# The forget sum of an attention's logits, moved from four-row matmuls into a zero row of the keys

## The chip, the cores and the metric

The program runs on one core of a Trainium2 chip: TensorE (PE; its weight loads are listed as PEld), VectorE (DVE), ScalarE (ACT), GpSimd (POOL) and SyncE (SP), which here only issues DMAs. The metric is the device time of one execution in microseconds (us).

## The reference

A sequence of 256 tokens with 1024 features passes two layers of a first block and two layers of a second one (gated linear recurrence and windowed attention). A layer of the first block is a SwiGLU, a mixer, and a SwiGLU. The mixer has four groups of 256 features each: differential attention, a convolution of 31 taps, a chunked spatial gate, and the forgetting attention, which is the one that is changed:

```python
def _forgetting_attention(q, k, v, log_f):      # four heads of 64
    cum = jnp.cumsum(log_f.astype(jnp.float32), axis=1)
    ...
        s = jnp.einsum('bqhd,bkhd->bhqk', qi, k).astype(jnp.float32) * scale
        s = s + jnp.transpose(ci, (0, 2, 1))[..., None] - cum_k[:, :, None, :]
        ...
        p = jax.nn.softmax(jnp.where(causal, s, NEG_INF), axis=-1)
        return jnp.einsum('bhqk,bkhd->bqhd', p.astype(v.dtype), v)
```

The term of the query's own position (`ci`) is the same for all keys, so the softmax drops it, and only the key's running sum is needed: one number for each head and key.

## The kernel before, in words

**Tiling.** Every large product is fp32 split into a high and a low part: three matmuls (L368 high by high, L369 activations' high by weights' low, L370 low by high) for each 128x512 product, summed in one PSUM bank. Weights stream from HBM in pieces of 512 KB (`wr`, issued on SP, three buffers). ScalarE casts each piece to its high part (`wh`, L336) and VectorE subtracts to get the low part (`wl`, L339), both into nine buffers.

**A mixer layer.** The input product yields column groups in the order conv, dqk, fqk, vv, gmlp. Each of the four mixer groups is a Python generator that is advanced between pieces of the large product, so that its small work stands among the weight matmuls. A scheduler with priorities then fixes the order on each engine, and an engine runs its list strictly in order. The output product takes the groups in the order differential attention, forgetting attention, spatial gate, convolution (`OUT1 = [0, 3, 2, 1]`), so it can't end before the convolution's features are there. The convolution's 62 taps (L875) run on VectorE wherever the order puts them. Behind them come transposes (L884), a layer norm (L845, L846, then L444 and small instructions), ScalarE's `L852`, transposes (L626), and a split into high and low (L336 on ScalarE, L339 on VectorE) for the output product. The weights of the spatial gate and its products (L917 to L920) come before that.

**The forgetting attention (`fox`).** q and k of a token half are normalised, transposed on PE (L489) and copied from PSUM by ScalarE: k to `kT` (L1033, two heads above one another in 128 partitions), q to `qm` (L1036) twice, each time multiplied by a column `mg` that is the gain in one head's 64 rows and zero in the other's. So the product of `qm` and `kT` over 128 rows holds one head alone. For each head PE adds into one PSUM bank the causal mask (L1046), the running sum `cum` (4 rows by 256, made by `decay`) by a matmul over four rows in which a broadcast column of the identity picks the head (L1049), and the product of q and k (L1051). `exp_rows` takes the row maximum on VectorE (L647) and the exponentials on ScalarE (L651). Small constants of all groups lie in one tile, `col_sb`, of 880 columns, loaded by one DMA at the start.

Of the kernel before, what the change touches and what calls it, by code (L numbers as in the profile page):

```python
# [9 lines left out]
F32 = mybir.dt.float32  # L10
# [3 lines left out]
AF = mybir.ActivationFunctionType  # L14
# [4 lines left out]
S, D, DEPTH, DFF = 256, 1024, 2, 2816  # L19
# [21 lines left out]
Z1 = [(n, Z1_COLS[n]) for n in ("conv", "dqk", "fqk", "vv", "gmlp")]  # L41
OUT1 = [0, 3, 2, 1]
MIX1 = ("diff", "conv", "gmlp", "fox")

_PERM = [(2048 + 64 * h, 2112 + 64 * h) for i in range(4) for h in (i, i + 4)]
Z2 = [
# [90 lines left out]
_F1 = {}  # L137
for _name, _n in [("ada_b", 144), ("norm_g", 48), ("conv_w", 124), ("conv_b", 4), ("conv_g", 4), ("conv_nb", 4),
                  ("dgq", 2), ("dgk", 2), ("dog", 2), ("fgq", 2), ("fgk", 2), ("bs", 8), ("fb", 2),
                  ("lam", 256), ("maskf", 2), ("ident", 128), ("tri", 128), ("hgain", 2), ("sink", 16)]:  # L140
    _off = sum(n for _, n in _F1.values())
    _F1[_name] = (_off, _n)
NCOL = sum(n for _, n in _F1.values())
# [2 lines left out]
def pack_cols(inp):  # L146
    out = np.zeros((128, NCOL), np.float32)

    def put(name, a):
        o, n = _F1[name]  # L150
        out[:a.shape[0], o:o + n] = a.reshape(a.shape[0], n)

    def fm(a):
        return a.reshape(-1, 128).T

    def rep(a, k):
        return np.concatenate([a] * k, axis=-1)

    put("ada_b", fm(inp["ada_b"]))
    put("norm_g", fm(inp["norm_g"]))  # L160
    put("conv_w", inp["conv_w"].reshape(2, TAPS, 2, 128).transpose(3, 0, 2, 1))
    put("conv_b", fm(inp["conv_b"]))
    put("conv_g", fm(inp["conv_norm_g"]))
    put("conv_nb", fm(inp["conv_norm_b"]))
    put("dgq", rep(inp["diff_qk_g"][:, 0], 4).T)
    put("dgk", rep(inp["diff_qk_g"][:, 1], 4).T)
    put("dog", rep(inp["diff_out_g"], 2).T)
    put("fgq", rep(inp["fox_qk_g"][:, 0], 2).T)
    put("fgk", rep(inp["fox_qk_g"][:, 1], 2).T)
    put("bs", inp["gmlp_bs"].transpose(2, 0, 1))  # L170
    put("fb", inp["fox_fb"].T)
    put("lam", np.broadcast_to(inp["diff_lambda"].reshape(1, 256), (128, 256)))
    p = np.arange(128)
    put("maskf", (p[:, None] // 64 == np.arange(2)[None]).astype(np.float32))
    put("ident", np.eye(128, dtype=np.float32))
    put("tri", (p[:, None] <= p[None, :]).astype(np.float32))
    put("hgain", inp["hgrn_head_gain_2"].T)
    sk = inp["attn_sinks_2"].reshape(1, 2, 2, 4).transpose(0, 1, 3, 2)
    put("sink", np.broadcast_to(sk.reshape(1, 16), (128, 16)))
    return out  # L180
# [43 lines left out]
def body(ctx, tc, ws, cols, x, c, adaw, wf, gmn, wst, bmask, lev, pred, sbias, gains, lbs, out, phases=range(12)):  # L224
    nc = tc.nc
    V, A, T = nc.vector, nc.scalar, nc.tensor
# [5 lines left out]
    def nm(p):  # L232
        uid[0] += 1
        return f"{p}{uid[0]}"

    def pool(name, bufs=1, stack=ctx, **kw):
        return stack.enter_context(tc.tile_pool(name=name, bufs=bufs, **kw))

    const = pool("const")
# [9 lines left out]
    def s2(shape=(128, 512), dt=F32):  # L249
        return s2_p.tile(list(shape), dt, tag="s2", name=nm("s"))  # L250

    def s1(shape=(128, 256), dt=F32):
        return s1_p.tile(list(shape), dt, tag="s1", name=nm("h"))

    def sm(n):
        return sm_p.tile([128, 32], F32, tag="sm", name=nm("m"))[:, 0:n]

    def tp(shape, dt=F32):
        return ps_p.tile(list(shape), dt, tag="ps", name=nm("t"))
# [13 lines left out]
    def C(name, i=0, n=None):  # L273
        o, w = _F1[name]
        return col_sb[:, o + i:o + (w if n is None else i + n)]

    ident = C("ident")
# [208 lines left out]
    def transposed(src):  # L486
        ps = tp([128, 4, 128])
        for j in range(4):
            T.transpose(ps[:, j], src[:, 128 * j:128 * j + 128], ident)  # L489
        return ps  # L490
# [138 lines left out]
    def bc(ap, n):  # L629
        return ap.unsqueeze(2).to_broadcast([ap.shape[0], ap.shape[1], n])  # L630

    def heads(ap, e):
        return ap.rearrange("p (g e) -> p g e", e=e)
# [21 lines left out]
    def keys_first(p):  # L655

        ps = tp([128, 4, 128])
        for i in range(4):
            T.transpose(ps[:, i], p[i], ident)
        pt = s2([128, 4, 128])  # L660
        A.copy(pt, ps)
        return pt
# [2 lines left out]
    first_block = ctx.enter_context(ExitStack())  # L665
    mod = [const.tile([128, 72], F32, name=f"mod{l}") for l in range(2)]
    an = [const.tile([128, 24], F32, name=f"an{l}") for l in range(2)]
    const.tile([128, 8], F32, name="trail")
    c1 = pool("c1", 1, first_block)
    ada_p = pool("ada", NA, first_block)  # L670
    cond = c1.tile([128, D], F32, name="cond")
# [154 lines left out]
    def mix1(ph):  # L826
        l = ph // 3
        got = {}
        mg, cvh, ypad = G1["mg"], G1["cvh"], G1["ypad"]
# [95 lines left out]
        def qk_norms(acc, group):  # L925

            n = 512 // group
            r = sm(2 * n)
            res = [s2(), s2()]
            for t in range(2):  # L930
                A.activation(res[t], acc[t], AF.Square)
                V.tensor_reduce(out=r[:, n * t:n * t + n], in_=heads(res[t], group), axis=AX.X, op=ALU.add)
            rsqrt(r, r, 1.0 / group)
            for t in range(2):
                V.tensor_tensor(out=heads(res[t], group), in0=heads(acc[t], group),
                                in1=bc(r[:, n * t:n * t + n], group), op=ALU.mult)
            return res
# [70 lines left out]
        def decay():  # L1008

            ps = tp([4, S])  # L1010
            wfh, wfl = G1["wf"]
            for k in range(8):
                mm3(ps, wfh[:, l, k], wfl[:, l, k], xh[:, k], xl[:, k], k == 0, k == 7)
            y, e, cum = s1()[0:4], s1()[0:4], s1()[0:4]
            fb = C("fb", l, 1)[0:4]
            V.tensor_scalar(out=y, in0=ps, scalar1=fb, scalar2=0.0, op0=ALU.add, op1=ALU.min)
            A.activation(e, ps, AF.Abs, bias=fb)
            A.activation(e, e, AF.Exp, scale=-1.0)
            A.activation(e, e, AF.Ln, bias=1.0)
            V.tensor_tensor(out=e, in0=e, in1=y, op=ALU.subtract)  # L1020
            V.tensor_tensor_scan(out=cum, data0=G1["ones"], data1=e, initial=0.0, op0=ALU.mult, op1=ALU.add)
            return cum

        def fox(acc):
            zs = qk_norms(acc, 64)
            cum = decay()
            yield
            yield
            kT = s2([128, 2, S])
            qm = []  # L1030
            for t in range(2):
                ps = transposed(zs[t])
                A.copy(kT[:, :, 128 * t:128 * t + 128], ps[:, 2:4])  # L1033
                q = s2([128, 2, 2, 128])
                for i in range(2):
                    A.activation(q[:, :, i], ps[:, 0:2], AF.Copy, scale=mg[:, l, 1 + i:2 + i])  # L1036
                qm.append(q)
            yield
            p, r = [[], []], []
            for t in range(2):  # L1040
                keys = 128 * (t + 1)
                per = 512 // keys
                sums = sm(4)
                for b in range(4 // per):
                    ps = tp([128, per, keys])
                    T.matmul(ps.rearrange("p a b -> p (a b)"), identb, G1["mask"][t], start=True, stop=False)  # L1046
                    for i in range(per):
                        g = b * per + i
                        T.matmul(ps[:, i], ident[0:4, g:g + 1].to_broadcast([4, 128]), cum[:, 0:keys], start=False,  # L1049
                                 stop=False)  # L1050
                        T.matmul(ps[:, i], qm[t][:, g // 2, g % 2], kT[:, g // 2, 0:keys], start=False,  # L1051
                                 stop=i == per - 1)
                    p[t] += exp_rows(ps, per, sm(per), sums, range(b * per, b * per + per))
                    yield
                r.append(sm(4))
                V.reciprocal(out=r[t], in_=sums)
            yield
            pts = [[keys_first([p[t][i][:, 128 * kt:128 * kt + 128] for i in range(4)]) for kt in range(t + 1)]
                   for t in range(2)]
            yield  # L1060
            while ("v", 0) not in got:
                yield
            o = [s1(), s1()]
            for t in range(2):
                ps = weighted(pts[t], [got["v", n][:, 256:512] for n in range(2)])
                V.tensor_tensor(out=heads(o[t], 64), in0=ps, in1=bc(r[t], 64), op=ALU.mult)
            yield
            got["fox"] = mixed_slot(to_features(o))
# [15 lines left out]
        def src(i):  # L1084
            name = MIX1[OUT1[i]]
            until(lambda: name in got)
# [413 lines left out]
```

## Time and profile before

| what | value |
|---|---|
| time, median of three runs | 2214.31 us (2215.36, 2205.01, 2214.31) |
| the profiled execution's time | 2208.89 us |
| its span in the trace | 2207.1 us |
| PE busy | 2149.9 us, 97% of the span |
| VectorE busy | 1486.1 us, 67% |
| ScalarE busy | 1191.5 us, 54% |
| mean granted TensorE clock | 0.991 |

The profiled execution's time is 1.8 us over its span, which begins with the first instruction on the engines. A matmul's listed length runs past the start of the next one, since they are pipelined. What a matmul costs PE is the distance from one start to the next. A granted clock of 1.00 is the full 2.4 GHz, 0.50 the lower level of 1.2 GHz.

### The profile page before, as it was taken

How to read it: one execution, taken by the hardware profiler on the slowest of the kernel's cores; microseconds unless marked ns; L12 is line 12 of the kernel's file. 1: busy time of each engine (PE TensorE's matmuls, PEld its weight loads, DVE VectorE, ACT ScalarE, POOL GpSimd, SP SyncE). 2: the span in 40 equal slices, each digit the busy share in tenths (PEclk: the TensorE clock that was granted, in tenths of full speed). 3: DMA queues.
4: the chain of work that ended last, by engine and by line, in shares of the span. 5: the costliest groups of instructions: out<-in, count | busy, mean ns of one | idle time of the engine just before them, and what ended most of it. 6: DMA issues, size and time to landing. Idle time of an engine off the chain costs nothing.

```text
span 2207.1 us, 27771 instructions
## 1 busy us (share of the span) xinstructions
PE 2149.9 (97%) x10148; PEld 1765.8 (80%) x10150; DVE 1486.1 (67%) x2224; ACT 1191.5 (54%) x1933; POOL 0.2 (0%) x4
## 2 busy tenths in 40 slices
PE   6999998999999999999999999999999999999998
PEld 5787776888888777888888888888888887887887
DVE  6788986765888786655754665675566557657653
ACT  6544656544544756553644565464465447556552
POOL 0000000000000000000000000000000000000000
PEclk9999998999999999999999999999999999999999
DMA  8889734885889533755755543475555555245652
GB/s 321 294 318 337 259 118 152 293 265 174 314 336 342 209 113 126 247 181 183 246 187 188 179 143 115 135 234 184 191 181 202 189 171 183 96 143 177 205 182 95
DMA packets 125416, 452.90 MB, mean 205 GB/s; under 512 B 14176, under 2 KB 14432, under 8 KB 125280
## 3 DMA queue, kind: packets, MB, share of 16 engines
q1 hardware_dynamic: 125280, 451.13, 59.2%
q8 instruction: 80, 1.31, 0.2%
q14 instruction: 56, 0.46, 0.1%
HBM read 450.03 MB, written 1.05 MB: 204 GB/s over the span
## 4 chain that ended last, share of the span: by engine, by line
PE 77%; DMA 8%; ACT 7%; DVE 6%; issue 2%; SPq 0%; DVEq 0%; ACTq 0%
PE a L368 23%; PE a L369 22%; PE a L370 22%; DMA wr<-in_ws 8%; ACT wh L336 3%; DVE wl L339 3%; PE t L626 2%; PE t L489 1%; PE t L1234 1%; ACT h L476 1%; DVE spill L683 1%; ACT s L533 1%; PE t L1188 1%; PE t L970 1%; PE t L1346 0%
## 5 line engine op out<-in xcount | busy, mean ns | idle before, releaser
L339 DVE TENSOR_TENSOR wl<-wr,wh 128x1024 fp32r<-128x1024 f32 x692 | 843.2, 1223 | 468.0 <-ACT wh L336 463.0
L336 ACT CAST wh<-wr 128x1024 fp32r<-128x1024 f32 x692 | 726.8, 1052 | 718.5 <-PE a L370 388.1
L368 PE MATMUL a<-wh,xh 128*128 128x512 f32 x1888 | 750.7, 398 | 7.9 <-ACT xh L534 6.0
L369 PE MATMUL a<-wl,xh 128*128 128x512 f32 x1888 | 736.4, 390 | 1.9 <-DVE wl L339 1.9
L370 PE MATMUL a<-wh,xl 128*128 128x512 f32 x1888 | 736.0, 391 | 0.0
L368 PEld LDWEIGHTS a<-wh,xh 128*128 128x128 f32 x1888 | 357.6, 189 | 81.6 <-ACT xh L534 6.7
L370 PEld LDWEIGHTS a<-wh,xl 128*128 128x128 f32 x1888 | 356.9, 189 | 75.5 <-DVE xl L339 1.4
L369 PEld LDWEIGHTS a<-wl,xh 128*128 128x128 f32 x1888 | 357.6, 189 | 73.0 <-DVE wl L339 3.7
L368 PE MATMUL a<-wh,s 128*128 128x512 f32 x896 | 352.2, 393 | 3.9 <-ACT s L336 2.8
L369 PE MATMUL a<-wl,s 128*128 128x512 f32 x896 | 350.8, 392 | 0.8 <-DVE wl L339 0.8
L370 PE MATMUL a<-wh,s 128*128 128x512 f32 x896 | 349.3, 391 | 0.0
L368 PEld LDWEIGHTS a<-wh,s 128*128 128x128 f32 x896 | 168.9, 188 | 39.8 <-ACT s L336 3.4
L369 PEld LDWEIGHTS a<-wl,s 128*128 128x128 f32 x896 | 168.9, 188 | 35.6 <-DVE wl L339 1.6
L370 PEld LDWEIGHTS a<-wh,s 128*128 128x128 f32 x896 | 168.7, 188 | 35.3 <-DVE s L339 0.6
L683 DVE CUSTOM_DVE_ANT_0 spill<-ada,cond 128x1024 bf16<-128x1024 f32 x144 | 175.5, 1219 | 5.9 <-DMA ada<-in_adaw 5.3
L489 PE MATMUL t<-col_sb,s 128*128 128x128 f32 x304 | 45.9, 285 | 27.3 <-ACT s L740 18.3
L489 PEld LDWEIGHTS t<-col_sb,s 128*128 128x128 f32 x304 | 35.1, 144 | 41.7 <-ACT s L740 19.1
L339 DVE TENSOR_TENSOR s<-t,s 128x512 fp32r<-128x512 f32 x96 | 64.9, 684 | 3.4 <-ACT s L336 3.4
L626 PE MATMUL t<-col_sb,h 128*128 128x128 f32 x392 | 58.9, 274 | 6.2 <-DVE h L594 3.2
L626 PEld LDWEIGHTS t<-col_sb,h 128*128 128x128 f32 x392 | 48.0, 141 | 19.6 <-DVE h L594 4.3
L590 ACT ACTIVATE h<-a,m 128x256 f32<-128x256 f32 x88 | 40.7, 473 | 36.4 <-PE a L370 36.3
L336 ACT CAST s<-t 128x512 fp32r<-128x512 f32 x96 | 54.9, 582 | 5.6 <-PE t L626 5.6
(241 smaller groups left out, 1251.5 us busy)
## 6 DMA issues: line engine op xcount, KB each, us to landing
wr<-in_ws SPq DMA_DIRECT2D x692, 512.0 KB, 4.0
ada<-in_adaw SPq DMA_DIRECT2D x144, 512.0 KB, 5.7
row<-in_gains SPq DMA_DIRECT2D x12, 512.0 KB, 4.9
h<-in_x SPq DMA_DIRECT2D x2, 512.0 KB, 7.3
out<-h SPq DMA_DIRECT2D x4, 256.0 KB, 2.0
cond<-in_c SPq DMA_DIRECT2D x1, 512.0 KB, 4.3
gmn<-in_gmn SPq DMA_DIRECT2D x2, 256.0 KB, 5.1
wst<-in_wst SPq DMA_DIRECT2D x2, 256.0 KB, 6.2
```

The costliest lines, as they stand in the source:

```text
L336: ins = A.copy(dst_h, src)
L339: return V.tensor_tensor(out=dst_l, in0=src, in1=dst_h.bitcast(F32), op=ALU.subtract)
L368: T.matmul(acc, a, wh, start=start, stop=False)
L369: T.matmul(acc, a, wl, start=False, stop=False)
L370: T.matmul(acc, b, wh, start=False, stop=stop)
L476: A.activation(junk, src, AF.Square, accum_out=ss[:, i:i + 1])
L489: T.transpose(ps[:, j], src[:, 128 * j:128 * j + 128], ident)
L533: A.activation(xt[:, j], ps[:, j], AF.Identity, scale=a, bias=b)
L590: A.activation(g, acc[t][:, 0:256], AF.Silu, scale=r)
L626: T.transpose(ps[:, i, 128 * t:128 * t + 128], src[t][:, 128 * i:128 * i + 128], ident)
L683: ins = V.tensor_tensor_reduce(out=spill, in0=raw, in1=cond, scale=1.0, scalar=0.0, op0=ALU.mult, op1=ALU.add, accum_out=mod[l][:, n:n + 1])
L970: T.matmul(ps[:, i], qT[rs, i, ts], kT[rs, i, 0:keys], start=False, stop=i == 1)
```

## The change

The running sum no longer has matmuls of its own. `qm` has rows that are zero for each head, and the product over 128 rows adds nothing there. In the changed kernel one of these rows holds a 1 in the queries and the running sum in the keys.

- There are two key tiles, one for even heads and one for odd ones, so `kT` is copied twice (four copies a layer, for two).
- `qm` is written by eight instructions of 128x128 a layer (scale and a bias column `frow`), for four of 128x256.
- One matmul over four rows (`frep`, 128 columns, 256 keys) writes the running sum of each head into 32 rows of a PSUM tile, and four ScalarE copies of 32x256 put them over zero rows of the keys (head 1 in rows 0 to 31, head 3 in 32 to 63, head 0 in 64 to 95, head 2 in 96 to 127).
- The eight matmuls of L1049 in a layer are gone. Every other product is as it was.
- `col_sb` has 1012 columns, for 880. A pad of 8 columns beside other constants is one of 4.

```diff
--- before
+++ after
+FOX_AT = (1, 3, 0, 2)
...
-                  ("lam", 256), ("maskf", 2), ("ident", 128), ("tri", 128), ("hgain", 2), ("sink", 16)]:
+                  ("lam", 256), ("maskf", 2), ("ident", 128), ("tri", 128), ("hgain", 2), ("sink", 16),
+                  ("frow", 4), ("frep", 128)]:
...
+    put("frep", (np.repeat(FOX_AT, 32)[None] == np.arange(4)[:, None]).astype(np.float32))
+    put("frow", (np.arange(128)[:, None] == 32 * np.argsort(FOX_AT)[None]).astype(np.float32))
...
-    const.tile([128, 8], F32, name="trail")
+    const.tile([128, 4], F32, name="trail")
...
-            kT = s2([128, 2, S])
+            kT = [s2([128, 2, S]) for _ in range(2)]
             qm = []
             for t in range(2):
                 ps = transposed(zs[t])
-                A.copy(kT[:, :, 128 * t:128 * t + 128], ps[:, 2:4])
                 q = s2([128, 2, 2, 128])
                 for i in range(2):
-                    A.activation(q[:, :, i], ps[:, 0:2], AF.Copy, scale=mg[:, l, 1 + i:2 + i])
+                    A.copy(kT[i][:, :, 128 * t:128 * t + 128], ps[:, 2:4])
+                    for n in range(2):
+                        A.activation(q[:, n, i], ps[:, n], AF.Identity, scale=mg[:, l, 1 + i:2 + i],
+                                     bias=C("frow", 2 * n + i, 1))
                 qm.append(q)
+            ps = tp([128, S])
+            T.matmul(ps, C("frep")[0:4], cum, start=True, stop=True)
+            for at, g in enumerate(FOX_AT):
+                rs = slice(32 * at, 32 * at + 32)
+                A.copy(kT[g % 2][rs, g // 2], ps[rs])
             yield
...
                         g = b * per + i
-                        T.matmul(ps[:, i], ident[0:4, g:g + 1].to_broadcast([4, 128]), cum[:, 0:keys], start=False,
-                                 stop=False)
-                        T.matmul(ps[:, i], qm[t][:, g // 2, g % 2], kT[:, g // 2, 0:keys], start=False,
+                        T.matmul(ps[:, i], qm[t][:, g // 2, g % 2], kT[g % 2][:, g // 2, 0:keys], start=False,
                                  stop=i == per - 1)
```

Line numbers behind the new lines move: L368 to L370 are L374 to L376 in the changed kernel, L336 and L339 are L342 and L345, L651 is L657, L1046 is L1060 and L1051 is L1063.

The scheduler moves other instructions with it. On PE in layer 0, where the logits of the first token half stand, before (`t_2485` is the PSUM tile of its four heads, `h_2348` the running sum, `a_...` the sums of the large product):

```order
L1046 MATMUL t_2485<-bm,identb 128x512
L1049 MATMUL t_2485<-h_2348,col_sb 128x128
L368 MATMUL a_2355<-wh_2231,xh 128x512
L369 MATMUL a_2355<-wl_2232,xh 128x512
L370 MATMUL a_2355<-wh_2231,xl 128x512
L368 MATMUL a_2356<-wh_2231,xh 128x512
L1051 MATMUL t_2485<-s_2428,s_2435 128x128
L1049 MATMUL t_2485<-h_2348,col_sb 128x128
L1051 MATMUL t_2485<-s_2428,s_2435 128x128
L1049 MATMUL t_2485<-h_2348,col_sb 128x128
L1051 MATMUL t_2485<-s_2428,s_2435 128x128
L1049 MATMUL t_2485<-h_2348,col_sb 128x128
```

and in the changed kernel (the first token half is now `t_2498`, the second half's first two heads `t_2539`):

```order
L973 LDWEIGHTS identb
L973 MATMUL t_2527<-bm,identb 128x512
L976 MATMUL t_2527<-s_2207,s_2208 128x256 x2
L1060 LDWEIGHTS identb
L1060 MATMUL t_2539<-bm,identb 128x512
L374 MATMUL a_2552<-wh_2359,xh 128x512
L375 MATMUL a_2552<-wl_2360,xh 128x512
L376 MATMUL a_2552<-wh_2359,xl 128x512
L1063 MATMUL t_2498<-s_2428,s_2435 128x128
L1063 MATMUL t_2498<-s_2429,s_2435 128x128
L1063 MATMUL t_2498<-s_2428,s_2435 128x128
L1063 MATMUL t_2498<-s_2429,s_2435 128x128
```

The four products of q and k stand close together now. The mask of their own tile (`t_2498`) is 12 weight matmuls, a differential block (L973, L976), the next tile's mask (L1060, here) and three weight matmuls ahead of the first of them. The new `frep` matmul stands further ahead, right behind the transposes of q and k.

On ScalarE at the same place of layer 0, before (`t_2429` and `t_2438` are the transposed q and k of the two token halves):

```order
L1033 COPY s_2428<-t_2429 128x2x128
L1036 ACTIVATE s_2435<-t_2429,mg 128x2x128 x2
L1033 COPY s_2428<-t_2438 128x2x128
L1036 ACTIVATE s_2444<-t_2438,mg 128x2x128 x2
L336 CAST wh_2555<-wr_2553 128x1024
L651 ACTIVATE s_2480,m_2393<-t_2475,m_2479 128x256 x2
```

and in the changed kernel (`t_2454` is the running sum spread over 32-row groups):

```order
L1042 COPY s_2428<-t_2430 128x2x128
L1044 ACTIVATE s_2435<-t_2430,col_sb,mg 128x128 x2
L1042 COPY s_2429<-t_2430 128x2x128
L1044 ACTIVATE s_2435<-t_2430,col_sb,mg 128x128 x2
L1042 COPY s_2428<-t_2442 128x2x128
L1044 ACTIVATE s_2447<-t_2442,col_sb,mg 128x128 x2
L1042 COPY s_2429<-t_2442 128x2x128
L1044 ACTIVATE s_2447<-t_2442,col_sb,mg 128x128 x2
L1051 COPY s_2429<-t_2454 32x256 x2
L1051 COPY s_2428<-t_2454 32x256 x2
L657 ACTIVATE s_2493,m_2393<-t_2488,m_2492 128x256 x2
L342 CAST wh_2562<-wr_2560 128x1024
```

Six instructions have become sixteen, and the weight cast that stood right behind them now stands behind two exponentials of the differential attention.

On VectorE at the convolution's layer norm in layer 1, before (`t_7302` is its transposed output, `s_7251` the low part of a group for the output product):

```order
L339 TENSOR_TENSOR wl_7339<-wr_7336,wh_7338 128x1024
L845 BN_STATS m_7310<-t_7302 128x6
L339 TENSOR_TENSOR s_7251<-t_7245,s_7250 128x512
L846 BN_AGGR m_7307<-m_7310 128x2
L845 BN_STATS m_7313<-t_7302 128x6
L846 BN_AGGR m_7307<-m_7313 128x2
L444 TENSOR_SCALAR m_7316<-m_7307 128x2
```

and in the changed kernel (there `t_7312`):

```order
L345 TENSOR_TENSOR wl_7303<-wr_7300,wh_7302 128x1024
L851 BN_STATS m_7320<-t_7312 128x6
L345 TENSOR_TENSOR s_7261<-t_7255,s_7260 128x512
L852 BN_AGGR m_7317<-m_7320 128x2
L851 BN_STATS m_7323<-t_7312 128x6
L345 TENSOR_TENSOR wl_7349<-wr_7346,wh_7348 128x1024
L852 BN_AGGR m_7317<-m_7323 128x2
L345 TENSOR_TENSOR wl_7355<-wr_7352,wh_7354 128x1024
L450 TENSOR_SCALAR m_7326<-m_7317 128x2
```

Two weight subtractions have moved in between the second statistics and the small instructions of the norm. Further ahead in layer 1, one more weight subtraction and one more tap stand ahead of the spatial gate's products than before. In layer 0, VectorE's four taps and a weight subtraction stand ahead of the first maximum of the forgetting attention, where the taps stood behind it. SP issues the same DMAs in nearly the same order.

## Rows read from the trace of the kernel before

**Rows 1.** The page's first line, busy times (part 1), GB/s of 40 slices (part 2).

```profile
span 2207.1 us, 27771 instructions
...
PE 2149.9 (97%) x10148; PEld 1765.8 (80%) x10150; DVE 1486.1 (67%) x2224; ACT 1191.5 (54%) x1933; POOL 0.2 (0%) x4
...
GB/s 321 294 318 337 259 118 152 293 265 174 314 336 342 209 113 126 247 181 183 246 187 188 179 143 115 135 234 184 191 181 202 189 171 183 96 143 177 205 182 95
```

**Rows 2.** Source view of L1049: durations in ns (min/median/max), first and last start.

```profile
L1049 PE MATMUL t<-h,col_sb x32: 270/374/577, 279.3 to 808.3; 4*128 4x128 f32 x16, 4*128 4x256 f32 x16
```

**Rows 3.** PE timeline, layer 0: start, length, engine, line, operation; two records a matmul.

```profile
279.31 0.48 PE L1049 MATMUL t<-h,col_sb 4*128 4x128 f32 x2
...
281.09 0.48 PE L1049 MATMUL t<-h,col_sb 4*128 4x128 f32 x2
281.50 0.49 PE L1051 MATMUL t<-s,s 128*128 128x128 f32 x2
...
285.34 0.39 PE L967 MATMUL t<-bm,identb 128*128 128x512 bf16 x1
...
287.03 0.69 PE L1049 MATMUL t<-h,col_sb 4*128 4x256 f32 x2
287.66 0.70 PE L1051 MATMUL t<-s,s 128*128 128x256 f32 x2
```

**Rows 4.** ScalarE timeline, layer 0; in brackets the idle time and what ended it.

```profile
229.71 1.85 ACT L533 ACTIVATE s<-t,mod,an 128x128 f32<-128x128 f32 x5 [2.02 <-PE t L489]
...
278.69 0.37 ACT L1033 COPY s<-t 128x256 f32<-128x256 f32 x1
...
282.21 1.04 ACT L336 CAST wh<-wr 128x1024 fp32r<-128x1024 f32 x1 [1.41 <-DMA wr<-in_ws]
```

**Rows 5.** VectorE timeline, layer 0.

```profile
283.69 0.69 DVE L647 TENSOR_REDUCE m<-t 128x4 f32<-128x512 f32 x1 [1.50 <-PE t L1051]
...
287.43 1.22 DVE L339 TENSOR_TENSOR wl<-wr,wh 128x1024 fp32r<-128x1024 f32 x1
...
322.95 2.06 DVE L875 SCALAR_TENSOR_TENSOR s<-ypad,col_sb,s 128x256 f32<-128x256 f32 x5
...
330.05 0.17 DVE L846 BATCH_NORM_AGGREGATE m<-m 128x2 f32<-128x6 f32 x1
```

**Rows 6.** PE timeline, end of layer 0's mixer.

```profile
334.56 0.44 PE L626 MATMUL t<-col_sb,h 128*128 128x128 f32 x2 [2.36 <-ACT h L852]
...
339.87 0.79 PE L368 MATMUL a<-wh,s 128*128 128x512 f32 x1 [2.77 <-ACT s L336]
...
345.15 0.39 PE L368 MATMUL a<-wh,s 128*128 128x512 f32 x1
345.38 0.40 PE L369 MATMUL a<-wl,s 128*128 128x512 f32 x1
```

**Rows 7.** Windows view: PE, PEld, DVE, ACT, POOL busy; granted clock; DMA share; GB/s.

```profile
790.00:800.00 10.00, 10.00 (x32) 7.04 (x32) 5.68 (x11) 3.75 (x14) 0.00 (x0) 0.66 0.30 106
```

**Rows 8.** PE timeline, layer 1's mixer.

```profile
790.44 0.48 PE L1049 MATMUL t<-h,col_sb 4*128 4x128 f32 x2
...
836.50 0.60 PE L884 MATMUL t<-col_sb,s 128*128 128x128 f32 x4
...
847.28 0.40 PE L368 MATMUL a<-wh,s 128*128 128x512 f32 x1
```

**Rows 9.** VectorE timeline, the convolution's normalisation in layer 1.

```profile
839.43 0.17 DVE L444 TENSOR_SCALAR m<-m 128x2 f32<-128x2 f32 x1
```

**Rows 10.** ScalarE timeline, layer 1.

```profile
787.12 0.37 ACT L1033 COPY s<-t 128x256 f32<-128x256 f32 x1
...
846.45 0.66 ACT L336 CAST s<-s 128x512 fp32r<-128x512 f32 x1
```

**Rows 11.** DMA issues: line, count, KB each, us from issue to landing.

```profile
col_sb<-in_cols SPq DMA_DIRECT2D x1, 440.0 KB, 8.2
```

**Rows 12.** ScalarE timeline, the start.

```profile
11.43 0.29 ACT L750 ACTIVATE mod<-mod,col_sb 128x1 f32<-128x1 f32 x1 [3.98 <-DMA col_sb<-in_cols]
```

## The prediction

> **What bounds the kernel now.** I read the busy times first: PE works 2149.9 of 2207.1 us, so only 57.2 us of the span are not matmuls [rows 1]. The bound is PE, and a change counts if it shortens what PE has to do or wait for. The source view then says how much of PE the change touches: 32 records of L1049, half of 128 columns and half of 256 [rows 2]. A matmul of these kinds leaves two records, so there are 16 matmuls, 8 a layer, 4 of each width. Next I read what stands around them. In layer 0 PE runs through them without a wait, and so in layer 1, but both times the mixer's end is near another limit. In layer 0 the output product waits twice for the convolution, 2.36 and 2.77 us, and PE then starts at the low clock: 12 matmuls from 339.87 to 345.15 take 0.44 each, where the next ones take 0.23 [rows 6]. In layer 1 the convolution's last cast ends at 847.11 and PE takes its first product with it at 847.28 [rows 8, 10], without a wait but with only 0.2 to spare. So the question is not what the matmuls cost, but what of it passes these two places.
>
> **PE: removed and added.** A four-row matmul of 128 columns costs 281.50 - 281.09 = 0.41 and one of 256 costs 287.66 - 287.03 = 0.63 [rows 3]. A layer loses 4 x 0.41 + 4 x 0.63 = 4.16 and gains one `frep` matmul of 4 rows and 256 columns, 0.63. Net 3.5 a layer, 7.1 in all. The products of q and k and the masks stay.
>
> **ScalarE: six instructions become sixteen.** The block of before begins at 278.69 and ends 1.41 before 282.21, at 280.80 [rows 4]: 2.11 for six instructions, 0.35 each. The eight new ones of 128x128 have a scale and a bias column; L533 has the same form and takes 1.85 / 5 = 0.37 [rows 4]. Copies of 32x256 aren't in the trace. They have the columns of a 128x256 copy, so I take 0.35 (below: a quarter of the partitions may cost less; above: 0.37, the listed length of a whole copy). Sum 16 x 0.35 = 5.6, at most 5.9. That is 3.5 more a layer on an engine that works 54% of the span, so it costs nothing unless PE comes to wait. In layer 0 the block ends at 284.3 to 284.6. PE gets to the first product of q and k later than before, since the order now puts it further back: 279.31, plus `frep` 0.63, 12 weight matmuls 2.76, the differential block and the next mask 287.03 - 285.34 = 1.69, three weight matmuls 0.69, is 285.1 [rows 3, 6]. Cover 0.5 to 0.8. In layer 1 the block begins at 787.12 and ends at 792.7 to 793.0. The logits, at 790.44 before, now stand behind `frep` and ten weight matmuls, so at about 793.4 [rows 6, 8, 10]. Cover 0.4 to 0.7. If the block were longer than 6.3, PE would wait one us for each further one, and the row maximum on VectorE with the taps behind it too. The weight cast at 282.21 now comes behind the block and two exponentials, at most 4 x 0.35 with the reading of their sums, so it ends by 287.0. Its subtraction ran at 287.43 before [rows 5] and stands behind the forgetting maximum now: still covered. The load that reuses its raw buffer starts later by as much; DMA has the room (a share of 0.30 in the stretch of rows 7).
>
> **Layer 0: what passes.** The convolution's tail runs on VectorE, which loses no work. Before, it waits 1.50 for the first forgetting maximum at 283.69 [rows 5]. In the new order four taps and a weight subtraction come ahead of that maximum; it waits until PE is through the four products, 285.1 + 3 x 0.41 and the 0.49 of the last one [rows 3], 286.8: some 2 us of wait. Following the new order from there with the durations of the rows, I get the last tap ending at 325.4 (325.0 before) and the norm's second aggregate at 329.6 (330.05 before), since one subtraction has left the way between them [rows 5]. PE's 3.5 us become a longer wait for the convolution, and what reaches the end is -0.5. Bounds: +0.5, if only the late tap counts, and -3.5, if all of PE's gain passed.
>
> **Layer 1: what passes.** PE's busy time hides a loss here: from 790 to 800 it is busy 10.00 of 10.00 us, but the granted clock is 0.66, so 3.4 us of work at full speed were lost in the midst of the four-row matmuls and 32-row products [rows 7]. There is no idle time in the stretch. What stood there is what the change takes out, and in the new order weight matmuls stand between the mask and the products, so I take it as gone. Then PE is 3.5 + 3.4 earlier. Against it, one more weight subtraction (1.22) and one more tap (2.06 / 5 = 0.41) stand ahead of the spatial gate's products on VectorE [rows 5], some 1.5 with their overlap: 5.4 left at L884, 836.50 before [rows 8]. From there on the limit is the convolution's chain of small steps, 836.50 to 847.11. In the new order two weight subtractions stand between its second statistics and the first small step of the norm, at 839.43 before [rows 9]: 2 x 1.2 = 2.4 by the 1.22 above. The chain's end comes 5.4 - 2.4 = 3.0 earlier, and PE waits for it. Gain 3.0. Bounds: 3.5 - 1.5 - 2.4 = -0.4, that is nothing, if the clock falls as before, and 6.9 if neither insertion matters.
>
> The Trainium skill ("TensorE: Matmul & The Clock Gate", section "Part 1: The HAM clock gate (the "warmup" mystery)") puts the low clock down to idle time on PE. The row of 790 to 800 shows it with no idle time, so here the trace doesn't bear the rule out; by the rule the change would give nothing of the 3.4 back, and the sum would come out at about the time before.
>
> **The start.** `col_sb` grows from 440 to 506 KB. Its load ends a wait of 3.98 of ScalarE at 11.43 [rows 11, 12]; it lands 8.2 after its issue. In proportion the 66 KB would be 1.2; at the 321 GB/s of the span's first slice [rows 1] they are 0.2. I take 0.2, since other loads share the 8.2.
>
> **Sum.** 2207.1 - 0.5 - 3.0 + 0.2 = 2203.8, and with the 1.8 that lie around the span 2205.6. The profiled time of before, 2208.89, lies 5.4 under the median of the runs shown, 2214.31, and 2.0 under the mean of all four times known, 2210.9. I add 2.0: **2207.6**.
>
> **Rivals.** Times have the same 2.0 added.
> - *All of it passes.* 7.1 and the 3.4 of the clock reach the end: 2208.9 - 10.5 + 0.2 + 2.0 = 2200.6. For it: PE is 97% busy. Against it: the convolution is the last operand in both layers, and PE already waits for it in one. Chance 0.12.
> - *Nothing passes.* The low clock comes in layer 1 as before or elsewhere, the two subtractions eat PE's rest, and layer 0 stays tied to the taps: 2208.9 + 2.0 = 2210.9. For it: the bound of layer 1 above, and the wait in layer 0. Against it: the order breaks up the run of narrow products. Chance 0.22. The rule of the Trainium skill named above leads here too.
> - *Slower, by the clock behind a longer wait.* In layer 0 PE is freed of 3.5 us only to wait longer for the convolution: 2.36 + 2.77 become some 8.1. The row behind the present wait shows 12 matmuls at half clock; 12 to 25 more of them at 0.21 are 2.6 to 5. With no gain in layer 1 that is 2213.5, up to 2216. Against the forecast's gain of 3.3 in all it decides from 3.3 / 0.21 = 16 further matmuls at the low clock. For it: the low clock stands right behind these waits. Against it: the first wait is as long already, and the clock can fall no lower. Chance 0.16.
>
> The Trainium skill's section "HAM oscillation — how this bites in real kernels" on the same page describes such gaps behind dependent stages, and the rows at 339.87 agree: the low clock follows the two waits.
>
> **How the numbers follow.** My forecast has 0.50: **2207.6**, by its bounds 2203 to 2212. The range takes in "all of it passes" and the slower rival: **2199 to 2216**, as the runs of one kernel spread over 10 us. A measurement tells 0.5%, 11 us, from no change here, so faster means under 2203.2. That needs most of the first rival (0.10 of its 0.12) and a low draw of the forecast (0.07): **0.17**. Slower, over 2225.4, no case reaches but by a wait that I overlooked: **0.03**. Same **0.80**.
>
> **What would show it.** PE's records fall by 28 (32 less, 4 new); ScalarE's block takes 5.6 and ends before the first product of q and k, which shows no wait. The granted clock of the stretch that answers to 790 to 800 is 1.00. PE's wait for the convolution in layer 0 grows by some 3, and in layer 1 there is a new one of 2 to 3 ahead of the first product with it. I am wrong if PE waits for ScalarE's small copies, if the stretch keeps its low clock, or if the last tap moves by more than 1 us.

## The result, and the profile after

The changed kernel takes 2226.45 us (median of four runs, 2225.78 to 2227.78), against 2211.84 for the kernel before: a ratio of 1.0072, 95% interval [1.0055, 1.0089]. It is slower by some 16 us, where 2207.6 was forecast, and it lies outside the range of 2199 to 2216.

The page of the changed kernel (span and busy times; compare [rows 1]):

```profile
span 2226.0 us, 27729 instructions
...
PE 2167.9 (97%) x10122; PEld 1759.2 (79%) x10122; DVE 1485.8 (67%) x2224; ACT 1196.6 (54%) x1953; POOL 0.2 (0%) x4
```

PE has 26 records less, 28 in the weight loads (PEld; a few matmul records are missing from a trace), and is busy 18.0 us longer. The span grew by 18.9. So the loss is not a wait: idle time of PE hardly changed (57.2 before, 58.1 now), and the same matmuls take longer. The lines view of PE shows which ones. Its columns are line, engine, operation, operands, shapes and count, then busy us and mean ns, then idle time ahead of them. After:

```profile
L374 PE MATMUL a<-wh,xh 128*128 128x512 f32 x1888 | 758.4, 402 | 7.8 <-ACT xh L540 6.0 <-ACT xh L760 1.8
L375 PE MATMUL a<-wl,xh 128*128 128x512 f32 x1888 | 744.3, 394 | 0.9 <-DVE wl L345 0.9
L376 PE MATMUL a<-wh,xl 128*128 128x512 f32 x1888 | 742.9, 394 | 0.0
L374 PE MATMUL a<-wh,s 128*128 128x512 f32 x896 | 353.5, 395 | 6.1 <-ACT s L342 5.5 <-ACT s L646 0.4
```

and before, which rows 1 to 12 don't hold:

```profile
L368 PE MATMUL a<-wh,xh 128*128 128x512 f32 x1888 | 750.7, 398 | 7.9 <-ACT xh L534 6.0 <-ACT xh L754 1.8
L369 PE MATMUL a<-wl,xh 128*128 128x512 f32 x1888 | 736.4, 390 | 1.9 <-DVE wl L339 1.9
L370 PE MATMUL a<-wh,xl 128*128 128x512 f32 x1888 | 736.0, 391 | 0.0
L368 PE MATMUL a<-wh,s 128*128 128x512 f32 x896 | 352.2, 393 | 3.9 <-ACT s L336 2.8 <-ACT s L640 0.9 <-ACT wh L336 0.2
```

In such a row the weights stand first and the activations second; the activations are the matmul's first operand, the one that TensorE loads ahead (PEld lists the load of `xh`, 128x128), and the 512 columns of weights are then streamed past them. The three matmuls of the triple whose first operand is `xh` or `xl` (the activations of every product that reads the residual stream) sum to 758.4 + 744.3 + 742.9 = 2245.6, for 2223.1 before. These are sums of lengths that overlap, so they say which matmuls grew and not by how much the span did. With `s` as first operand nearly nothing changed (353.5 for 352.2 in the first of the three). These matmuls are spread over the whole program, most of them far from the mixers that the change edits. In the second block, where no line was changed, the timeline of PE shows 12 steps from one L370 to the L370 four triples on (1502.10 to 1504.82), 2.72 us, 0.2267 a step:

```profile
1502.10 0.39 PE L370 MATMUL a<-wh,xl 128*128 128x512 f32 x1
...
1504.59 0.39 PE L369 MATMUL a<-wl,xh 128*128 128x512 f32 x1
1504.82 0.39 PE L370 MATMUL a<-wh,xl 128*128 128x512 f32 x1
```

and in the changed kernel 12 steps between two L376 take 2.80, 0.2333 a step:

```profile
1503.76 0.40 PE L376 MATMUL a<-wh,xl 128*128 128x512 f32 x1
...
1506.33 0.39 PE L375 MATMUL a<-wl,xh 128*128 128x512 f32 x1
1506.56 0.40 PE L376 MATMUL a<-wh,xl 128*128 128x512 f32 x1
```

There is no wait in either stretch, and the granted clock from 1500 to 1510 is 1.00 in both. A step that is 3% longer in thousands of matmuls is the whole loss and more.

In the mixers, most of what the prediction looked for is there. The new ScalarE work in layer 0:

```profile
278.39 0.37 ACT L1042 COPY s<-t 128x256 f32<-128x256 f32 x1
...
282.19 1.49 ACT L1051 COPY s<-t 32x256 f32<-32x256 f32 x4
283.71 0.47 ACT L657 ACTIVATE s<-t,m 128x256 f32<-128x256 f32 x1
```

The block runs from 278.39 to the next exponential at 283.71, 5.3 us. PE has the `frep` matmul at 274.74 and gets to the first product of q and k at 284.96, without a wait:

```profile
274.74 0.69 PE L1048 MATMUL t<-h,col_sb 4*128 4x256 f32 x2
...
284.96 1.92 PE L1063 MATMUL t<-s,s 128*128 128x128 f32 x12
```

At the mixer's end PE waits longer for the convolution, 4.24 and 2.87 (compare [rows 6]):

```profile
333.67 0.90 PE L632 MATMUL t<-col_sb,h 128*128 128x128 f32 x4 [4.24 <-ACT h L858]
...
338.92 0.80 PE L374 MATMUL a<-wh,s 128*128 128x512 f32 x1 [2.87 <-ACT s L342]
```

and in layer 1 there is a new wait for it, 2.66, with half-clock steps of 0.43 behind it until 849.89 (seven from 846.90 on take 2.99; compare [rows 8]):

```profile
846.23 0.49 PE L374 MATMUL a<-wh,s 128*128 128x512 f32 x1 [2.66 <-ACT s L342]
...
846.90 0.63 PE L374 MATMUL a<-wh,s 128*128 128x512 f32 x1
...
849.89 0.48 PE L374 MATMUL a<-wh,s 128*128 128x512 f32 x1
```

The granted clock in the stretch that was at 0.66 before [rows 7] is 1.00:

```profile
780.00:790.00 10.00, 10.00 (x45) 6.84 (x44) 9.95 (x25) 6.57 (x16) 0.00 (x0) 1.00 0.31 107
790.00:800.00 10.00, 10.00 (x46) 7.21 (x46) 8.46 (x17) 8.85 (x31) 0.00 (x0) 1.00 0.33 107
800.00:810.00 10.00, 10.00 (x52) 8.21 (x51) 9.90 (x23) 7.62 (x22) 0.00 (x0) 1.00 0.34 107
```

### The profile page after: what moved, and what is told of

It is laid out like the page before. It is cut to its first block, busy times and chain, and to the rows that moved or that the text cites. A ratio compares the mean times of both kernels' runs of the same rounds, so it can differ in the third digit from the quotient of the medians.

```text
span 2226.0 us, 27729 instructions
## 1 busy us (share of the span) xinstructions
PE 2167.9 (97%) x10122; PEld 1759.2 (79%) x10122; DVE 1485.8 (67%) x2224; ACT 1196.6 (54%) x1953; POOL 0.2 (0%) x4
## 4 chain that ended last, share of the span: by engine, by line
PE 80%; DMA 6%; ACT 6%; DVE 5%; issue 2%; SPq 0%; DVEq 0%; ACTq 0%
PE a L374 24%; PE a L376 24%; PE a L375 24%; DMA wr<-in_ws 6%; ACT wh L342 2%; DVE wl L345 2%; PE t L632 2%; PE t L495 1%; PE t L1246 1%; ACT h L482 1%; DVE spill L689 1%; PE t L1200 1%; ACT s L539 1%; PE t L976 1%; PE t L1358 0%
## 5 line engine op out<-in xcount | busy, mean ns | idle before, releaser
L345 DVE TENSOR_TENSOR wl<-wr,wh 128x1024 fp32r<-128x1024 f32 x692 | 842.9, 1223 | 486.3 <-ACT wh L342 483.2
L342 ACT CAST wh<-wr 128x1024 fp32r<-128x1024 f32 x692 | 725.2, 1051 | 716.4 <-PE a L376 399.9
L374 PE MATMUL a<-wh,xh 128*128 128x512 f32 x1888 | 758.4, 402 | 7.8 <-ACT xh L540 6.0
L375 PE MATMUL a<-wl,xh 128*128 128x512 f32 x1888 | 744.3, 394 | 0.9 <-DVE wl L345 0.9
L376 PE MATMUL a<-wh,xl 128*128 128x512 f32 x1888 | 742.9, 394 | 0.0
L374 PEld LDWEIGHTS a<-wh,xh 128*128 128x128 f32 x1888 | 356.3, 189 | 91.3 <-ACT xh L540 6.7
L376 PEld LDWEIGHTS a<-wh,xl 128*128 128x128 f32 x1888 | 355.3, 188 | 85.3 <-DVE xl L345 0.8
L374 PE MATMUL a<-wh,s 128*128 128x512 f32 x896 | 353.5, 395 | 6.1 <-ACT s L342 5.5
L376 PE MATMUL a<-wh,s 128*128 128x512 f32 x896 | 350.2, 392 | 0.0
L374 PEld LDWEIGHTS a<-wh,s 128*128 128x128 f32 x896 | 169.5, 189 | 42.8 <-ACT s L342 6.7
L376 PEld LDWEIGHTS a<-wh,s 128*128 128x128 f32 x896 | 169.3, 189 | 35.6 <-DVE s L647 0.5
L345 DVE TENSOR_TENSOR s<-t,s 128x512 fp32r<-128x512 f32 x96 | 65.0, 684 | 3.8 <-ACT s L342 3.8
L342 ACT CAST s<-t 128x512 fp32r<-128x512 f32 x96 | 55.1, 584 | 16.6 <-PE t L632 16.6
```

Of the source, the lines that this page charges most:

```text
L342: ins = A.copy(dst_h, src)
L345: return V.tensor_tensor(out=dst_l, in0=src, in1=dst_h.bitcast(F32), op=ALU.subtract)
L374: T.matmul(acc, a, wh, start=start, stop=False)
L375: T.matmul(acc, a, wl, start=False, stop=False)
L376: T.matmul(acc, b, wh, start=False, stop=stop)
```

## The experiments

What had moved beside the work were the addresses. In the built program (the addresses stand in no trace) `col_sb` grows from 3520 to 4048 bytes a partition, the next tile begins at a multiple of 32, 4064 on, and the pad of 8 columns takes 32 bytes as the one of 4 does. So every buffer behind them lies 544 bytes higher, 512 and 32: `xh` still begins at byte 16896, a multiple of 512, but the first `wh` buffer at 58912, for 58368, 32 off a multiple of 512. The split activations `s` lie behind `col_sb` too and moved with the weights. That fits the lines above: where both operands moved (`s`) nearly nothing changed, where only the weights moved (`xh`, `xl`) the step grew. The address theory is tried against the theory that the new work or its order costs the time.

**Realigned.** The changed kernel, with the pad left out (so 512 bytes of shift, not 544):

```diff
-    const.tile([128, 4], F32, name="trail")
```

> The changed kernel without its pad of 4 columns, so that all working buffers move down by 32 bytes: they then lie 512 bytes above those of before, at multiples of 512 as the activations xh and xl do. Work and order are as in the changed kernel. Address theory (a weight matmul is slower when its weights in SBUF lie 32 bytes off the place, modulo 512, of the activations): the spacing of the matmuls of xh and xl falls back from 0.233 to 0.2274 us; 3 x 1888 of them by 0.0057 are 32 us, so about 2195. Work theory (the new work or its order costs the time): 2226 as the changed kernel.

Measured: 2208.29 median, ratio to before 0.9977 [0.9962, 0.9992]. The lines view:

```profile
L374 PE MATMUL a<-wh,xh 128*128 128x512 f32 x1888 | 750.4, 398 | 8.2 <-ACT xh L540 6.0 <-ACT xh L760 1.8 <-ACT wh L342 0.3
L375 PE MATMUL a<-wl,xh 128*128 128x512 f32 x1888 | 736.2, 390 | 1.4 <-DVE wl L345 1.4
L376 PE MATMUL a<-wh,xl 128*128 128x512 f32 x1888 | 735.8, 391 | 0.0
```

The three lines are back at 750.4, 736.2 and 735.8, as before the change. The work theory falls. The size was 18, not 32. PE's busy time falls by 25.3 (2167.9 to 2142.6), but it idles 65.7 us here (span 2208.3), 7.6 more than in the changed kernel. That would fit other engines keeping their pace while the matmuls get faster; no run tests it.

**The kernel before, shifted.**

```diff
-    const.tile([128, 8], F32, name="trail")
+    const.tile([128, 144], F32, name="trail")
```

> The kernel before with its pad of 8 columns made 144, so that all working buffers lie where they lie in the changed kernel (544 bytes higher), with the work of before. Address theory: spacing 0.233 for the matmuls of xh and xl, 32 us more than before, about 2243. Work theory: no change, about 2212.

Measured: 2235.46, ratio 1.0096 [1.0073, 1.0119], with the same instructions in the same order as before:

```profile
L368 PE MATMUL a<-wh,xh 128*128 128x512 f32 x1888 | 760.7, 403 | 7.9 <-ACT xh L534 6.0 <-ACT xh L754 1.8
L369 PE MATMUL a<-wl,xh 128*128 128x512 f32 x1888 | 747.6, 396 | 1.3 <-DVE wl L339 1.3
L370 PE MATMUL a<-wh,xl 128*128 128x512 f32 x1888 | 745.6, 396 | 0.0
```

2253.9 for 2223.1. Here PE's busy time does grow by the 32 us of the sum (2149.9 to 2181.7), the span by 27.7 and the median by 22 (from 2213.44); the profiled execution of the kernel before, 2208.89, lies 4.5 under that median. So by the ratio the addresses alone cost some 21 us, and 1.0096 x 0.9977 = 1.0073, about the 1.0072 of the change.

**Both operands moved.**

```diff
-    const.tile([128, 96], F32, name="lead")
+    const.tile([128, 104], F32, name="lead")
...
-    const.tile([128, 4], F32, name="trail")
```

> The changed kernel with the pad ahead of xh and xl 8 columns longer and the other pad gone: activations and working buffers all lie at 32 modulo 512. If only the places of the two operands against each other count: spacing 0.2274, about 2195. If the place of the weights itself counts (32 off a multiple of 64): 0.233, about 2226.

Measured: 2211.10, ratio 0.9982 [0.9967, 0.9998]. Being 32 off a multiple of 512 costs nothing in itself (the 2195 that was expected takes the whole 32 us off once more). What counts is where weights and activations lie against each other.

**64 bytes**, from the changed kernel:

```diff
-    const.tile([128, 4], F32, name="trail")
+    const.tile([128, 16], F32, name="trail")
```

> The changed kernel with its pad of 4 columns made 16: working buffers at 64 modulo 512, activations at 0. If an odd multiple of 32 bytes is what costs: about 2195, spacing 0.2274. If every distance but a multiple of 512 costs: about 2226, spacing 0.233.

Measured: 2216.02, ratio 1.0011 [0.9997, 1.0026]: neither case, some 8 us over the realigned kernel.

**The activations `s` moved alone**, from the realigned kernel:

```diff
+    pool("gap").tile([128, 8], F32, name="gap")
     s2_p = pool("s2", NS2)
```

> The realigned changed kernel with a gap of 32 bytes between the weight buffers and the small working buffers: weights and xh, xl at multiples of 512, the split activations s (first operand of the second products of the SwiGLUs and of the mixers' output products) at 32. Pair theory (a matmul pays when its own two operands lie 32 apart modulo 512): 3 x 896 matmuls of s go from 0.2273 to 0.233, 15 us, about 2223; those of xh and xl stay at 0.2274. Rival (only xh and xl, which lie in another pool, are touched by it): no change, about 2208.

Measured: 2222.41, ratio 1.0041 [1.0016, 1.0065], as the pair theory had it: the triples of `s` slow down now, and those of `xh` don't.

**The low weights moved alone**, from the realigned kernel:

```diff
+    pool("gap1").tile([128, 8], F32, name="gap1")
     wl_p = pool("wl", NW)
+    pool("gap2").tile([128, 120], F32, name="gap2")
```

> The realigned changed kernel with the low weights wl alone 32 bytes off (a gap of 32 bytes ahead of them, 480 behind). Pair theory: only the second matmul of each triple (activations' high part by weights' low part) slows down, by 0.0057 in 1888 + 896 of them, 16 us, about 2224; first and third stay at 0.2274. Rival (the place of the next matmul's operand, or of all buffers together, decides): the slowdown shows in the first or third one, or in none (2208).

Measured: 2235.58, ratio 1.0105 [1.0084, 1.0127], 27 us over the realigned kernel, where 16 were expected. The lines (here L376 to L378 are the triple):

```profile
L376 PE MATMUL a<-wh,xh 128*128 128x512 f32 x1888 | 755.9, 401 | 8.3 <-ACT xh L542 6.2 <-ACT xh L762 2.0
L377 PE MATMUL a<-wl,xh 128*128 128x512 f32 x1888 | 749.3, 397 | 1.0 <-DVE wl L347 1.0
L378 PE MATMUL a<-wh,xl 128*128 128x512 f32 x1888 | 736.3, 391 | 0.0
```

The one with `wl` is slowest (749.3 for 736.2), but the first of the triple, whose own operands lie well, has grown too (755.9 for 750.4). From one start to the next it takes 231.8 ns behind the first, 235.1 behind the one with `wl` and 229.7 behind the third (those with `xh` and `xl`), all for some 227.5 in the realigned kernel. So a matmul's own pair is not the whole of it; that part of the pair theory fell.

Another pairing is a rival that no run was built to test. The load of a matmul's activations is listed at the start of the matmul ahead of it (in the stretch of the changed kernel above, the load for the L374 at 1504.00 starts at 1503.76, with the L376). So the weights that are being streamed and the activations that are being loaded for the next matmul could be the pair that counts. Where the first operand changes from `s` to `xh`, or from `xl` to `s`, the two readings differ (steps from the unrounded starts). In the changed kernel the step from the last `s` to the first `xh` takes 235 ns at all six places, and the one from the last `xl` to the first `s` 226 to 232 at ten. With `s` moved alone, the step from `xl` to `s` takes 235 at all ten. That is for the pair of stream and load. But the step from `s` to `xh` takes 232 to 236 there, which is for a matmul's own pair. So neither reading holds alone.

**128 and 256 bytes**, from the changed kernel, the first of them:

```diff
-    const.tile([128, 4], F32, name="trail")
+    const.tile([128, 32], F32, name="trail")
```

> The changed kernel with its pad at 32 columns: all working buffers 128 bytes off xh and xl modulo 512. At 64 bytes the spacing was 0.2285 to 0.230 for xh and xl. If the cost falls off with the distance from an odd multiple of 32: 0.2274, about 2208. If any distance but 512 costs as 64 does: about 2216.

Measured: 2227.55, ratio 1.0064 [1.0039, 1.0089]: as bad as 32, which neither case had. With 64 columns, 256 bytes:

> The changed kernel with its pad at 64 columns: working buffers 256 bytes off modulo 512. Same two cases as at 128: about 2208, or about 2216; a third, that 512 is not the period and 256 is worse: above 2216.

Measured: 2212.71, ratio 0.9997 [0.9984, 1.0011], with the step of the aligned kernels. It lies 4 us over the realigned one, but the two intervals overlap. In the profiled executions the mean granted clock is 0.988 here and 0.990 there, which is worth some 4 us.

The table gives the mean step between neighbouring weight matmuls, worked out from all rows of PE's timeline (some 7700 steps a kernel, those of 0.20 to 0.26 us, so at the full clock), by the first operand:

| kernel | bytes between weights and xh / s, modulo 512 | step, xh and xl (ns) | step, s (ns) | ratio to before |
|---|---|---|---|---|
| before | 0 / 0 | 227.5 | 227.1 | 1 |
| changed | 32 / 0 | 233.2 | 227.2 | 1.0072 |
| realigned | 0 / 0 | 227.5 | 227.1 | 0.9977 |
| before, shifted | 32 / 0 | 233.2 | 227.2 | 1.0096 |
| both at 32 | 0 / 0 | 227.4 | 227.0 | 0.9982 |
| 64 | 64 / 0 | 229.2 | 227.1 | 1.0011 |
| s off | 0 / 32 | 227.4 | 233.3 | 1.0041 |
| wl off | 32 for wl, 0 for wh / the same | 232.2 | 232.5 | 1.0105 |
| 128 | 128 / 0 | 232.6 | 227.3 | 1.0064 |
| 256 | 256 / 0 | 227.5 | 227.1 | 0.9997 |

The remaining four ask about the mixers. **Half the taps**, in the kernel before and in the realigned one:

```diff
-                for i in range(2):
+                for i in range(2 if k % 2 == 0 else 0):
                     w = C("conv_w", 62 * l + 31 * i + k, 1)
```

> The kernel before with every second tap of the convolution left out (32 of 62 remain in a layer), to make the convolution early. Read together with the next one. In both theories well under before: layer 0's mixer (219.0 to 350.0 before) loses its waits of 5.1 and the 2.5 of half clock behind them.

Measured: 2207.37, ratio 0.9978 [0.9960, 0.9997]. Layer 0's mixer takes 124.0 us, 7.0 less than with all taps, and no wait for the convolution is left in it.

> The realigned changed kernel with the same taps left out. If the convolution hides a part of what the change frees on TensorE (2.2 us shorter in layer 0's mixer where 3.5 were freed, and a new wait of 2.7 in layer 1): without that cover this one is 7 to 10 us under the one with half the taps of before, 3.5 of it in layer 0's mixer. If the part is lost to something else (the clock, ScalarE's new work): 4 to 5 us under, as with all taps.

Measured: 2197.12, ratio 0.9925 [0.9897, 0.9953]: 10.3 under the one before it, where the two differ by some 5 with all taps (0.9977). The intervals of the two ratios with half the taps, added as squares, leave some 4 to 19 us for that difference, so the times alone don't tell 10 from 5. Between 310 and the end of layer 0's mixer at 337.48 this kernel's PE has one wait listed, 0.65, and none for the convolution:

```profile
322.03 0.73 PE L376 MATMUL a<-wh,s 128*128 128x512 f32 x2 [0.65 <-DVE s L345]
...
337.48 1.33 PE L495 MATMUL t<-col_sb,s 128*128 128x128 f32 x8 [1.90 <-DVE s L518]
```

Layer 0's mixer takes 119.1 us here and 124.0 in the other (between the starts of the transposes on both sides of it), 4.9 less, against 2.2 less with all taps (131.0 to 128.8). That fits the convolution hiding a part. The rest need not be cover: the other kernel runs 15 us of layer 1 at a granted clock of 0.63 to 0.69, in the midst of its four-row matmuls, and loses some 5 us by it in the profiled execution, whose 2213.66 lies 6 over the median of that kernel:

```profile
790.00:795.00 5.00, 5.00 (x17) 3.74 (x17) 2.46 (x6) 1.66 (x10) 0.00 (x0) 0.63 0.32 105
795.00:800.00 5.00, 5.00 (x15) 3.10 (x14) 2.66 (x7) 1.41 (x4) 0.00 (x0) 0.69 0.01 2
800.00:805.00 5.00, 5.00 (x14) 3.30 (x14) 3.59 (x10) 2.33 (x9) 0.00 (x0) 0.66 0.34 105
```

**No running sum at all**, the kernel before without its four-row matmuls:

```diff
-                        T.matmul(ps[:, i], ident[0:4, g:g + 1].to_broadcast([4, 128]), cum[:, 0:keys], start=False,
-                                 stop=False)
```

> The kernel before without the four-row matmuls, the running sum left out of the logits: TensorE loses 4.16 a layer, ScalarE has no new work, addresses as before. If ScalarE's 3.3 more a layer and the frep matmul cost no more than their 0.63: about as the realigned changed kernel, 0.9977 of before, or up to 1.3 us under it. If the ScalarE block holds anything up: 3 us or more under it.

Measured: 2208.87, ratio 0.9973 [0.9958, 0.9987], as the realigned kernel. So no cost of ScalarE's new work shows, to within some 3 us, the width of the intervals. The same stretch of layer 1 has the full clock:

```profile
790.00:795.00 5.00, 5.00 (x27) 3.71 (x25) 5.00 (x13) 4.55 (x15) 0.00 (x0) 1.00 0.00 0
795.00:800.00 5.00, 5.00 (x27) 3.88 (x26) 4.45 (x8) 2.57 (x13) 0.00 (x0) 1.00 0.45 133
800.00:805.00 5.00, 5.00 (x23) 3.61 (x22) 4.50 (x10) 4.64 (x15) 0.00 (x0) 1.00 0.20 79
```

**Taps first**, the realigned kernel with the two lines of a tap under a higher priority:

```diff
-                for i in range(2):
...
+                with sooner(40):
+                    for i in range(2):
...
```

> The realigned changed kernel with the taps moved ahead by 40 in the scheduler's priorities. If the convolution is what the mixers wait for, its features come earlier, the waits of 4.4 and 2.5 in layer 0 and 2.7 in layer 1 shrink, and it ends at 2202 to 2206. Rival: the taps hold up the weight subtractions and the row maxima on VectorE, TensorE waits for those, and nothing is gained (2208) or lost.

Measured: 2201.76, ratio 0.9949 [0.9930, 0.9968], the fastest of the kernels that leave nothing out. Of the two waits in layer 0 one is left, and the mixer takes 122.6 (220.29 to 342.84); in layer 1 the wait is 1.51, for 2.66. A part of the rival shows too: a wait for VectorE at 308.60 is 1.89, where the realigned kernel's is 0.85. The rows of layer 0:

```profile
335.13 0.50 PE L374 MATMUL a<-wh,s 128*128 128x512 f32 x1 [2.72 <-ACT s L342]
...
342.84 1.06 PE L495 MATMUL t<-col_sb,s 128*128 128x128 f32 x8 [1.99 <-DVE s L518]
```

In the realigned kernel both stood there, and it took 128.8 (218.81 to 347.64):

```profile
332.20 1.03 PE L632 MATMUL t<-col_sb,h 128*128 128x128 f32 x4 [4.41 <-ACT h L858]
...
337.45 0.79 PE L374 MATMUL a<-wh,s 128*128 128x512 f32 x1 [2.51 <-ACT s L342]
...
347.64 1.07 PE L495 MATMUL t<-col_sb,s 128*128 128x128 f32 x8 [1.83 <-DVE s L518]
```

## Why the prediction was wrong

**The step that failed** is "The start". It priced the larger `col_sb` as a load alone, 0.2 us, and the pad as nothing, without a reason for the pad. The load did cost as little: ScalarE goes on at 11.64, for 11.43 [rows 12].

```profile
11.64 0.29 ACT L756 ACTIVATE mod<-mod,col_sb 128x1 f32<-128x1 f32 x1 [4.02 <-DMA col_sb<-in_cols]
```

What it left out is that a tile's size sets the address of everything behind it. 544 bytes of shift put the weights 32 bytes off the place of `xh` and `xl`, and lengthened 3 x 1888 matmuls by 0.0057 us each. That product is 32 us; alone the shift costs 21 us (before, shifted), or 18 on top of the change. None of the rivals had it, and the chance of 0.03 for a slower kernel was for an overlooked wait, where the loss is no wait. Both sizes stood in the diff.

**The other terms**, with the addresses put right, came out near their sum: 0.9977 is 5.1 us less (1.8 to 8.4), and the forecast had 3.3 less. That is luck in part, since layer 0 gave more and layer 1 less than was taken. The parts below come from one execution of each kernel; in these two, the unedited work behind layer 1 takes 5.4 us longer in the realigned kernel, 3.4 of it by a low clock from 1275 to 1282 that the other one lacks there.

- *PE's removed work.* Right. PE's busy time in the realigned kernel is 7.3 us less than before (2142.6 for 2149.9), for 7.1 worked out; what the clock does is in both. Without any running sum the kernel gains as much (0.9973), though no work was added there.
- *ScalarE's block.* 5.3 us, for 5.6 worked out; it ends before PE needs it in both layers. In layer 1 of the changed kernel its last copies end at 795.63 (794.14 + 1.49) and the first product stands at 796.88, by the same timelines.
- *Layer 0.* The wait for the convolution grew, but less than worked out (6.9 in the realigned kernel, for 8.1), and the mixer gained 2.2 (131.0 to 128.8) where 0.5 was taken, within its bounds of +0.5 and -3.5. The last tap ends at 323.2 there, for 325.0 before and 325.4 worked out. That is more than the 1 us that the prediction named as a sign of being wrong: what reaches the end of layer 0 was mis-sized, to the good.
- *Layer 1.* The low clock of 790 to 800 is gone and a wait of 2.66 for the convolution has come, as forecast. What I didn't price is the half clock behind that wait. From 350.02 to 854.84 it took 504.8 before and 503.0 in the realigned kernel (347.64 to 850.63), 1.8 less where 3.0 was taken.
- *The rivals.* "All of it passes" was wrong by its own reason, that the convolution is the last operand: layer 0's mixer gains 4.9 with half the taps and 2.2 with all. "Nothing passes" was wrong in that the low clock didn't come back in layer 1's four-row stretch. "Slower, by the clock behind a longer wait" named a real cost, the half clock behind the waits, but in layer 1, and it was some 1.6 us (nine steps from 846.23 to 849.89 take 3.66, for 2.1 at 0.23). The Trainium skill's page "TensorE: Matmul & The Clock Gate", section "HAM oscillation — how this bites in real kernels", describes matmuls that run at the lower level behind a gap on TensorE, there a wait for a DMA. The rows at 846.23 to 849.89 agree, behind a wait of 2.66 for ScalarE.

The rows of before that these spans rest on, the transposes at the ends of the two mixers:

```profile
219.02 1.07 PE L489 MATMUL t<-col_sb,s 128*128 128x128 f32 x8 [0.56 <-DVE s L512]
...
350.02 1.06 PE L489 MATMUL t<-col_sb,s 128*128 128x128 f32 x8 [1.95 <-DVE s L512]
...
854.84 1.11 PE L489 MATMUL t<-col_sb,s 128*128 128x128 f32 x8 [1.67 <-DVE s L512]
```

and, in the realigned kernel, the last taps of layer 0 and the end of layer 1's mixer:

```profile
320.76 2.45 DVE L881 SCALAR_TENSOR_TENSOR s<-ypad,col_sb,s 128x256 f32<-128x256 f32 x6
...
850.63 1.11 PE L495 MATMUL t<-col_sb,s 128*128 128x128 f32 x8 [1.87 <-DVE s L518]
```

**Still open.** How the low clock comes about in the four-row matmuls with PE busy throughout, which pair of weights and activations it is that counts, and what the two share in SBUF that 0 and 256 bytes apart cost nothing, 64 little, and 32 and 128 most. The steps were measured; a cause below them was not.

## What to carry to other kernels

A change to a constant's size or to a pad moves every buffer behind it. List the addresses of the operands of the commonest matmul before and after such a change, and compare them against each other (here modulo 512). When the busy time of an engine grows while its instructions get fewer, compare the step of one unchanged instruction far away from the edit first: here a few rows of an unedited stretch showed a loss that stood in no wait.

## What the runs showed of the hardware that was not expected

- The step of an fp32r matmul of 128x512 went from 227 ns to as much as 233 ns with the distance, modulo 512, between the SBUF addresses of weights and activations: 0 and 256 bytes 227.5, 64 bytes 229.2, 128 bytes 232.6, 32 bytes 233.2. These distances don't tell whether the period is 512 or 256. With only the low weights 32 off, its neighbours in the triple, whose own operands lie well, slow as well (231.8 and 229.7, for 235.1 with the low weights).
- In layer 1 the granted clock fell to 0.66 with PE busy all the time, in all three kernels that have the four-row matmuls: before (790 to 800), half the taps (790 to 805), and before, shifted, whose window is below. It stayed at 1.00 in that stretch in the changed kernel, in the realigned one and in the one without a running sum. In layer 0 the same matmuls ran at 1.00 in the kernel before, so they are not the whole of the reason; with half the taps the clock fell there too (0.66 from 285 to 290), again without a wait.

```profile
800.00:810.00 10.00, 10.00 (x32) 7.05 (x32) 4.92 (x11) 4.42 (x14) 0.00 (x0) 0.66 0.29 99
```
